# A one-core transformer step: six PSUM banks in turn in the merge and the output projection, norm diagonals on ScalarE, statistics of the second norm two slices later

## The chip, the cores and the metric

The kernel runs on one NeuronCore of a Trainium2 chip. The metric is the device time of one launch in microseconds (us), lower is better. Before the change three timed runs gave 1827.52, 1832.23 and 1832.83 us; their median is 1832.23 us.

## What is computed

One trunk layer of a hybrid diffusion backbone in fp32, for 128 context tokens and 1024 latent tokens (1152 in all), width 1024:

```
h   = rmsnorm(x, w1) * (1 + scale1) + shift1
q, k, v, u, g = h @ w_in                     # 4 heads, differential attention; conv input u; gates g
attn = head_norm(softmax(q1 k1) v - lam * softmax(q2 k2) v) @ w_attn_proj
conv = silu(layernorm(dwconv31(glu(u)))) @ w_conv_proj
m   = sigmoid(g[:1024]) * attn + sigmoid(g[1024:]) * conv
x   = x + gate1 * (m @ w_out)
h   = rmsnorm(x, w2) * (1 + scale2) + shift2
up  = dwconv3(h @ w_up)                      # 2 x 2816 channels
x   = x + gate2 * ((silu(up[:2816]) * up[2816:]) @ w_down)
y   = rmsnorm(x, w_final)
```

The six modulation vectors come from `silu(c) @ w_ada + b_ada`, for the context and for the latent conditioning.

## The kernel before

**Layout.** Activations stand transposed: 128 channels on the partitions, tokens along the row. The 1152 tokens are cut into three column groups n = 0, 1, 2 of 384 (CH). A tensor of width 1024 is eight chunks k of 128 channels.

**Matmuls.** To keep fp32 accuracy every operand is split in a high and a low part; `mm3` (line 196) issues three matmuls per chunk (high x high, high x low, low x high). One output block of 128 x 384 is a *unit*: 24 matmuls over eight chunks. The weights stream in a fixed order: SyncE (SP) loads a raw tile, ScalarE (ACT) makes the high part (line 153), GpSimd (POOL) the low part (line 155).

**PSUM.** There are eight banks. `banks` (line 284) makes the tags f (two banks), T (two) and O (one), and S (three banks in one tile). In attention S holds the scores. `any5` (line 293) hands out f, T, O, f, T in turn. At the start of `merge` (line 1043) one S tile is taken as `spare`: `spare[:, 0]` becomes `self.st`, the bank for norm statistics, and `spare[:, 1:3]` is a junk output for a reduction (`ada2`, line 1152).

**Ticks.** `run` (line 209) advances a clock, one tick after every eight matmuls of a unit (`mm3`'s yields, three ticks a unit of the output projection). `defer(t, f)` calls f at the tick now + t, so the number decides where in the written order the instructions of f stand. After that the framework's planner, which simulates the engines with its own costs, may still move instructions: an instruction that it thinks is not ready lets later ones pass. `pin` (line 296) bounds how far (on PE 144 places, on DVE 24).

**A norm's statistics.** Four steps: `stat_cols` (line 218) sums squares over the partitions with tiny matmuls into a PSUM bank, VectorE (DVE) adds EPS (line 228, tile `ms`), POOL takes the power -1/2 (line 230, `rs`). `stat_diag` (line 234) multiplies the 128 x 128 identity by one column of `rs` per 128 tokens (line 238, tile `dg`, up to three instructions). `stat_bcast` (line 242) multiplies a matrix of ones by `dg`, which puts the row of factors on all partitions in a PSUM bank. The consumers then read that bank. `stat_diag` serves the first norm (three groups), the conv layernorm in the last half of attention (`ln_jobs`, five groups, nine instructions in all), the second norm (three) and the final norm (three): 36 instructions.

**Merge** (lines 1084 to 1127). For each of eight output chunks j and each n: 12 matmuls into one bank (conv part), 12 into the next (attention part). DVE multiplies each by its gate tile `tg` (line 1110) and adds them (line 1112), ACT makes the high part `mh` (line 1114), POOL the low part `ml` (line 1116; DVE for j = 7). `tg` has two buffers; the load for the slice two further on is issued on SP's queue after that (line 1118), since it overwrites the buffer which `ml` has just read. Between the slices DVE runs `ada2` (line 1159): reductions over 1024 elements that make the later modulation vectors.

**Output projection** (`wo_unit`, line 1236). First pass: for j = 0..7 the units of n = 0 and 1. After each unit DVE adds the gated result to x1 (`resid`, line 1186), ACT squares it (line 1196) and DVE adds the square to `acc[n]` (line 1197). Second pass: j = 0..7 for n = 2. In the second pass the statistics and the normalisation of n = 0 and 1 are slipped in with `defer` (line 1261): a = `stat_cols`, a2 = `stat_diag`, b = `stat_bcast`, c0..c3 = `modnorm` (line 249: DVE multiplies, lines 253 and 261, ACT makes the high part, line 259, DVE and POOL the low part, line 267). Then the MLP (`ffn_body`, line 1273) begins, and n = 2 is normalised in its first units. The MLP's results go through ACT (line 1284) to `up`, and DVE's depthwise conv reads them (lines 1289 and 1291).

Of the kernel before, what the change touches and what calls it, by code (L numbers as in the profile page):

```python
# [10 lines left out]
AF = mybir.ActivationFunctionType  # L11
ALU = mybir.AluOpType
# [68 lines left out]
def _w_order():  # L81
    order = ["q0", "k0", "ua0", "ub0", "ua1", "ub1", "v0", "v1", "v2", "v3"]
    fill = FILL_SEQ.split()
    tail = [f"g{i}" for i in range(16) if f"g{i}" not in fill]
    merge = [f"m{j}" for j in range(8)]
    wo = [f"wo{j}" for j in range(8)]
    ffn = []
    done = 0
    for i in range(NFF):
        ffn += [f"fa{i}", f"fb{i}"]  # L90
        if i >= 2 and i % 2 == 0 and i < NFF - 2:
            ffn += [f"d{done}_0", f"d{done}_1"]
            done += 1
    while done < NFF // 2:
        ffn += [f"d{done}_0", f"d{done}_1"]
        done += 1
    return order, fill, tail, merge, wo, ffn
# [15 lines left out]
class Kernel:  # L113
# [120 lines left out]
    def stat_diag(self, rs, nt):  # L234
        nc = self.nc
        dg = self.sm.tile([128, CH], F32, tag="dg", name="dg", bufs=2)
        for t in range(nt):
            nc.vector.tensor_scalar(out=dg[:, t * 128:(t + 1) * 128], in0=self.ident,
                                    scalar1=rs[:, t:t + 1], scalar2=None, op0=ALU.mult)
        return dg  # L240

    def stat_bcast(self, dg, nt, psum):
# [41 lines left out]
    def banks(self, pool):  # L284

        def tag(t, n):
            return lambda: pool.tile([128, 512], F32, tag=t, name=t, bufs=n)

        self.fps, self.tps, self.ops = tag("f", 2), tag("T", 2), tag("O", 1)
        self.sps = lambda: pool.tile([128, 3, 512], F32, tag="S", name="S")  # L290
        self.five = cycle((self.fps, self.tps, self.ops, self.fps, self.tps))

    def any5(self):
        return next(self.five)()
# [748 lines left out]
    def merge(self):  # L1043
        tc, nc, A = self.tc, self.nc, self.A
        mh = [None] * NCH
        ml = [None] * NCH
        with tc.tile_pool(name="p2", bufs=1) as p2:
# [3 lines left out]
                xl.append(p2.tile([128, 8, CH], F32R, name=f"col{n}"))  # L1051

            self.gate_tile = lambda: self.sm.tile([128, CH], F32, tag="dg", name="gate", bufs=2)
            fps = self.any5
            spare = self.sps()
            self.st = lambda: spare[:, 0]
            self.junk = spare[:, 1:3]

            with tc.tile_pool(name="p2a", bufs=1) as p2a:
# [24 lines left out]
            with tc.tile_pool(name="p2b", bufs=1) as p2b:  # L1084
# [13 lines left out]
                for j in range(KC):  # L1098
                    wh, wl = self.take(f"m{j}")
                    for n in range(NCH):  # L1100
# [8 lines left out]
                        for s, ps in ((1, pc), (0, pa)):  # L1109
                            nc.vector.scalar_tensor_tensor(out=tg[:, s], in0=tg[:, s], scalar=1.0, in1=ps[:, :CH],  # L1110
                                                           op0=ALU.add, op1=ALU.mult)
                        nc.vector.scalar_tensor_tensor(out=tg[:, 0], in0=tg[:, 1], scalar=0.5, in1=tg[:, 0],
                                                       op0=ALU.mult, op1=ALU.add)
# [52 lines left out]
    def out_and_ffn(self):  # L1166
        tc, nc, A = self.tc, self.nc, self.A
        vec = self.vec
        with tc.tile_pool(name="p3", bufs=1) as p3:
            x1 = [p3.tile([128, KC, CH], F32, name=f"x1_{n}") for n in range(NCH)]  # L1170

            def load_x(n, q):
                nc.scalar.dma_start(out=x1[n][:, 2 * q:2 * q + 2], in_=A["xT"][n][:, 2 * q:2 * q + 2])

            load_x(0, 0)
            load_x(1, 0)

            fps, st = self.any5, self.st

            def bc8(v):  # L1180
                return v.rearrange("p (k o) -> p k o", o=1).to_broadcast([128, KC, 2])

            def resid(n, j, ps, gate):
                for o, ln, c in self.segs(n):
                    d = x1[n][:, j, o:o + ln]
                    nc.vector.scalar_tensor_tensor(out=d, in0=ps[:, o:o + ln], scalar=gate[:, j, c:c + 1], in1=d,  # L1186
                                                   op0=ALU.mult, op1=ALU.add)

            acc = [p3.tile([128, CH], F32, name=f"acc{n}") for n in range(NCH)]

            def square(n, j):
                if j == 0:
                    nc.scalar.activation(out=acc[n], in_=x1[n][:, 0], func=AF.Square)
                else:
                    sq = self.sm.tile([128, CH], F32, tag="dg", name="sq", bufs=2)
                    nc.scalar.activation(out=sq, in_=x1[n][:, j], func=AF.Square)
                    nc.vector.tensor_tensor(out=acc[n], in0=acc[n], in1=sq, op=ALU.add)

            hh = [None] * NCH
            hl = [None] * NCH  # L1200

            flip = [0]

            def mn():
                flip[0] += 1
                t = p3a.tile([128, 1156], F32, tag=("ya", "yb")[flip[0] % 2], name="mn")
                return t[:, :2 * CH].rearrange("p (k t) -> p k t", k=2)

            def h2(n, pool):
                hh[n] = self.hb.tile([128, KC, CH], F32R, tag="hb", name=f"h2h{n}")  # L1210
                hl[n] = self.hb.tile([128, KC, CH], F32R, tag="hb", name=f"h2l{n}")
                box = {}

                def a():
                    box["rs"] = self.stat_cols(acc[n], 3, st)

                def b():
                    box["r"] = self.stat_bcast(box["dg"], 3, st)

                def c(q):  # L1220
                    def f():
                        self.modnorm(n, 2 * q, 2, x1[n], box["r"][:, :CH], self.s2, self.h2s, hh[n], hl[n], pool,
                                     lambda i: i == 1 and n < 2)
                    return f

                def a2():
                    box["dg"] = self.stat_diag(box["rs"], 3)
                return [a, a2, b] + [c(q) for q in range(4)]

            with tc.tile_pool(name="p3a", bufs=1) as p3a:  # L1230
                self.start_ada2([p3a.tile([128, T], F32R, tag="fh", name=f"cbd{c}", bufs=4)[:, :1024].bitcast(F32)
                                 for c in range(2)],
                                lambda: p3a.tile([128, T], F32R, tag="fl", name="araw", bufs=4)[:, :1024].bitcast(F32))
                self.ada_fetch(2)

                def wo_unit(j, ns):
                    wh, wl = self.take(f"wo{j}")
                    for n in ns:
                        ps = fps()
                        self.run(self.mm3(ps[:, :CH], self.unit_ops(wh, wl, n, self.mh, self.ml), 8))  # L1240
                        resid(n, j, ps, self.g1)
                        square(n, j)
                        if n == ns[0]:
                            self.prep_to(self.late_prep)

                for j in range(KC):
                    if j % 2 == 0 and j < 6:
                        load_x(0, j // 2 + 1)
                        load_x(1, j // 2 + 1)
                    if j >= 4:  # L1250
                        load_x(2, j - 4)
                    wo_unit(j, (0, 1))
                    for _ in range(2):
                        if self.ada_raw:
                            self.ada2(1, self.ada_fetched < 24)
                nc.vector.tensor_copy(self.h2s, self.mod[:, 1])
                nc.vector.tensor_scalar(out=self.s2, in0=self.mod[:, 2], scalar1=1.0, scalar2=None, op0=ALU.add)
                nc.vector.tensor_tensor(out=self.s2, in0=self.s2, in1=bc8(vec[:, V_N2:V_N2 + 8]), op=ALU.mult)
                st0, st1 = h2(0, mn), h2(1, mn)
                for i, f in enumerate(st0 + st1):  # L1260
                    self.defer(1 + i + i // 2, f)
                for j in range(KC):
                    wo_unit(j, (2,))
                self.fetch_ahead = 2
                self.flush()
                for i, f in enumerate(h2(2, mn)):
                    self.defer(i // 2 + 1, f)
                self.ada_fetch(2)
                self.bg = [lambda: self.ada2(1)] * 8 + [lambda: nc.vector.tensor_copy(self.g2, self.mod[:, 3])]
                self.bg_rate = (1, 5)  # L1270
                self.ffn_body(p3, fps, st, x1, hh, hl, resid, square, acc, p3a)
# [289 lines left out]
```

## Time and profile before

| | us |
|---|---|
| median of three runs | 1832.23 |
| profiled execution, its own time | 1829.33 |
| span of the profiled execution, first to last instruction | 1827.2 |
| PE busy | 1723.0 (94%) |
| DVE busy | 1206.4 (66%) |
| POOL busy | 719.0 (39%) |
| ACT busy | 605.2 (33%) |

PE is TensorE, whose weight loads (PEld) run beside the matmuls; DVE is VectorE, ACT ScalarE, POOL GpSimd, SP SyncE. "idle <- X" names what the engine waited for last. The span is cut below into stages by time: the merge lies at 742 to 866 us, the output projection at 856 to 971 us, the MLP from there to the end.

### The profile page before, as it was taken

What the parts mean: (1) busy time and instruction counts of PE and PEld (TensorE: products, weight loads), DVE (VectorE), ACT (ScalarE), POOL (GpSimd) and SP (SyncE); (2) the same over time, 40 slices, a digit from 0 to 9 for tenths busy, and PEclk for the clock granted to TensorE, in tenths of its full rate; (3) what the DMA queues carried; (4) which work ended last, traced back from release to release, by engine and by line L of the source; (5) the groups of instructions that cost most, each with busy time, mean ns of one, the idle gap of its engine ahead of it and who ended that gap; (6) DMA issues with size and microseconds to landing.
All of it is one profiled execution on the core that took longest, in us unless ns stands there. A gap on an engine that the chain in (4) does not pass through costs nothing.

```text
span 1827.2 us, 25202 instructions
## 1 busy us (share of the span) xinstructions
PE 1723.0 (94%) x10138; PEld 1681.9 (92%) x10138; DVE 1206.4 (66%) x1515; ACT 605.2 (33%) x1097; POOL 719.0 (39%) x466
## 2 busy tenths in 40 slices
PE   5989889989989999899989999999999999999997
PEld 3889889988989999889989999999999999999997
DVE  5868985697796663687888855463554535545466
ACT  4424444354454553311243312222121221221222
POOL 2545782673873422644353422222222322322231
PEclk8999999999999999899999999999999999999998
DMA  8264233423325424665832211111111111111102
GB/s 312 80 186 143 91 94 88 151 78 118 116 76 184 138 87 166 224 212 176 283 113 58 93 35 47 43 39 47 37 46 47 35 47 47 35 47 47 35 24 104
DMA packets 86172, 184.05 MB, mean 101 GB/s; under 512 B 8196, under 2 KB 56232, under 8 KB 84008
## 3 DMA queue, kind: packets, MB, share of 16 engines
q1 hardware_dynamic: 33888, 101.27, 17.0%
q10 hardware_dynamic: 51592, 79.08, 13.6%
q0 software_dynamic: 576, 2.10, 0.3%
q8 instruction: 80, 1.31, 0.3%
q14 instruction: 36, 0.29, 0.1%
HBM read 142.80 MB, written 39.60 MB: 100 GB/s over the span
## 4 chain that ended last, share of the span: by engine, by line
PE 58%; DVE 19%; issue 5%; POOL 4%; DMA 2%; ACT 2%; ACTq 0%; POOLq 0%; DVEq 0%
PE f L203 25%; PE T L203 19%; PE O L203 9%; DVE conv L611 6%; DVE S L1159 2%; DVE mx L753 2%; PE O L794 2%; DVE e L766 2%; DMA tg<-scr_gscr 2%; DVE atl L783 1%; PE T L779 1%; PE S L746 1%; PE S L747 1%; POOL ml L1116 1%; POOL wlo L155 1%
## 5 line engine op out<-in xcount | busy, mean ns | idle before, releaser
L155 POOL TENSOR_TENSOR wlo<-raw,whi 128x1024 fp32r<-128x1024 f32 x123 | 311.5, 2534 | 619.8 <-ACT whi L153 518.2
L203 PE MATMUL f<-h1h,whi 128*128 128x384 f32 x680 | 232.6, 344 | 4.7 <-ACT gt L574 3.4
L203 PE MATMUL f<-h1l,whi 128*128 128x384 f32 x680 | 233.7, 344 | 0.0
L203 PE MATMUL f<-h1h,wlo 128*128 128x384 f32 x680 | 230.9, 340 | 0.0
L153 ACT CAST whi<-raw 128x1024 fp32r<-128x1024 f32 x125 | 131.0, 1048 | 283.9 <-PE f L203 114.7
L611 DVE SCALAR_TENSOR_TENSOR conv<-glu,vec,conv 128x967 f32<-128x967 f32 x120 | 199.2, 1660 | 1.1
L1289 DVE TENSOR_SCALAR ya<-up,vec 128x1153 f32<-128x1153 f32 x22 | 54.1, 2459 | 175.7 <-ACT up L1284 175.7
L203 PE MATMUL T<-h2h,whi 128*128 128x384 f32 x432 | 144.3, 334 | 0.0
L203 PE MATMUL T<-h2l,whi 128*128 128x384 f32 x432 | 144.3, 334 | 0.0
L203 PE MATMUL T<-h2h,wlo 128*128 128x384 f32 x432 | 144.1, 334 | 0.0
L624 POOL TENSOR_TENSOR conv<-conv,tap 128x200 f32<-128x200 f32 x120 | 115.6, 963 | 68.4 <-ACT tap L618 65.9
L203 PE MATMUL f<-h2h,whi 128*128 128x384 f32 x416 | 139.7, 336 | 2.6 <-ACT up L1284 2.6
L203 PE MATMUL f<-h2h,wlo 128*128 128x384 f32 x416 | 139.5, 335 | 0.0
L203 PE MATMUL f<-h2l,whi 128*128 128x384 f32 x416 | 139.3, 336 | 0.0
L203 PEld LDWEIGHTS f<-h1h,whi 128*128 128x128 f32 x680 | 129.5, 191 | 6.8 <-ACT gt L574 4.1
L203 PEld LDWEIGHTS f<-h1l,whi 128*128 128x128 f32 x680 | 130.1, 191 | 0.4
L203 PEld LDWEIGHTS f<-h1h,wlo 128*128 128x128 f32 x680 | 129.3, 190 | 0.2
L1305 POOL TENSOR_TENSOR fl<-ya,fh 128x128 fp32r<-128x128 f32 (+1 forms) x44 | 64.9, 1476 | 154.1 <-ACT fh L1304 154.1
L753 DVE TENSOR_REDUCE mx<-S 128x1 f32<-128x1152 f32 (+1 forms) x72 | 88.7, 1231 | 31.1 <-PE S L747 31.1
L1186 DVE SCALAR_TENSOR_TENSOR x<-f,g,x 128x384 f32<-128x384 f32 (+2 forms) x154 | 74.9, 505 | 48.6 <-PE f L203 45.5
L755 ACT ACTIVATE e<-S,mx 128x1152 f32<-128x1152 f32 (+1 forms) x72 | 81.2, 1128 | 70.1 <-DVE mx L753 62.7
L1289 DVE TENSOR_SCALAR yb<-up,vec 128x1153 f32<-128x1153 f32 x22 | 54.3, 2469 | 70.6 <-ACT up L1284 70.6
(332 smaller groups left out, 4646.3 us busy)
## 6 DMA issues: line engine op xcount, KB each, us to landing
raw<-in_wst SPq DMA_DIRECT2D x126, 512.0 KB, 3.5
araw<-in_ada ACTq DMA_DIRECT2D x32, 512.0 KB, 3.9
scr_gscr<-gate ACTq DMA_DIRECT2D x48, 192.0 KB, 2.0
tg<-scr_gscr SPq DMA_DIRECT2D x24, 384.0 KB, 4.1
ada<-in_ada SPq DMA_DIRECT2D x8, 1024.0 KB, 9.9
K<-scr_kscr ACTq DMA_DIRECT2D x4, 1920.0 KB, 8.8
V<-scr_vscr ACTq DMA_DIRECT2D x4, 1280.0 KB, 6.5
scr_vscr<-e ACTq DMA_DIRECT2D x36, 128.0 KB, 1.9
```

The costliest lines, as they stand in the source:

```text
L153: nc.scalar.copy(hi, raw)
L155: eng.tensor_tensor(out=lo, in0=raw, in1=hi.bitcast(F32), op=ALU.subtract)
L203: nc.tensor.matmul(out, lhsT=a, rhs=b, start=(i == 0), stop=(i == n - 1))
L611: t = nc.vector.scalar_tensor_tensor(out=o, in0=glu[:, j:j + CSPLIT], scalar=w[:, j:j + 1], in1=o, op0=ALU.mult, op1=ALU.add)
L624: t = nc.gpsimd.tensor_tensor(out=o, in0=o, in1=p, op=ALU.add)
L753: nc.vector.tensor_reduce(out=mx[:, 1:2], in_=src, axis=AX.XY, op=ALU.min)
L755: nc.scalar.activation(out=e[:, :w].rearrange("p (a b) -> p a b", a=nk), in_=src, func=AF.Exp, scale=-1.0, bias=mx[:, 1:2], accum_out=self ...
L766: nc.vector.scalar_tensor_tensor(out=e0[:, :w], in0=e1[:, :w], scalar=m1[:, 3:4], in1=e0[:, :w], op0=ALU.mult, op1=ALU.add)
L794: nc.tensor.matmul(o_ps[:, :w], lhsT=a, rhs=b, start=(i == 0), stop=(i == n - 1))
L1186: nc.vector.scalar_tensor_tensor(out=d, in0=ps[:, o:o + ln], scalar=gate[:, j, c:c + 1], in1=d, op0=ALU.mult, op1=ALU.add)
L1289: nc.vector.tensor_scalar(out=y[:, :L], in0=u[:, 0:L], scalar1=w[:, 0:1], scalar2=None, op0=ALU.mult)
L1305: nc.gpsimd.tensor_tensor(out=fl[:, d:d + ln], in0=ya[:, s:s + ln], in1=fh[:, d:d + ln].bitcast(F32), op=ALU.subtract)
```

## The change

Four edits. (1) `stat_diag` makes the diagonals with a ScalarE activation (Copy with a per-partition scale) instead of a VectorE multiply, in all 36 places. (2) A cycle `six` of f, T, O, f, T and `spare[:, 0]` hands out the accumulation banks from the end of the gate projections to the end of the output projection. (3) In the output projection the statistics and the broadcast of the second norm for n = 0 and 1 take their banks from that same cycle instead of always `spare[:, 0]`; before the MLP both names go back to what they were. (4) The deferred steps for n = 0 and 1 come two ticks later.

```diff
     def stat_diag(self, rs, nt):
...
-            nc.vector.tensor_scalar(out=dg[:, t * 128:(t + 1) * 128], in0=self.ident,
-                                    scalar1=rs[:, t:t + 1], scalar2=None, op0=ALU.mult)
+            nc.scalar.activation(out=dg[:, t * 128:(t + 1) * 128], in_=self.ident, func=AF.Copy,
+                                 scale=rs[:, t:t + 1])
...
+    def any6(self):
+        return next(self.six)()
...
-            fps = self.any5
             spare = self.sps()
             self.st = lambda: spare[:, 0]
+            self.six = cycle((self.fps, self.tps, self.ops, self.fps, self.tps, self.st))
+            fps = self.any6
             self.junk = spare[:, 1:3]
...
-            fps, st = self.any5, self.st
+            fps, st = self.any6, self.any6
...
                 for i, f in enumerate(st0 + st1):
-                    self.defer(1 + i + i // 2, f)
+                    self.defer(3 + i + i // 2, f)
                 for j in range(KC):
                     wo_unit(j, (2,))
                 self.fetch_ahead = 2
                 self.flush()
+                fps, st = self.any5, self.st
```

## Rows read from the trace of the kernel before

**Rows 1.** The page: busy us of each engine, its share of the span, instructions.
```profile
PE 1723.0 (94%) x10138; PEld 1681.9 (92%) x10138; DVE 1206.4 (66%) x1515; ACT 605.2 (33%) x1097; POOL 719.0 (39%) x466
```

**Rows 2.** Busy time of each engine by stage: stretch, its length, then busy us (instructions) of PE, PEld, DVE, ACT, POOL, then granted clock, DMA share, GB/s.
```profile
590.00:710.00 120.00, 118.60 (x763) 117.09 (x762) 72.64 (x111) 63.93 (x122) 37.97 (x39) 1.00 0.33 105
742.00:866.00 124.00, 111.16 (x600) 107.07 (x599) 95.54 (x144) 25.79 (x38) 57.18 (x34) 0.96 0.59 191
886.00:927.00 41.00, 38.18 (x221) 37.86 (x219) 39.23 (x60) 9.51 (x15) 14.06 (x5) 1.00 0.62 200
927.00:965.00 38.00, 32.37 (x175) 31.75 (x176) 30.85 (x46) 17.03 (x30) 23.37 (x13) 0.89 0.34 99
965.00:1022.00 57.00, 54.25 (x310) 53.61 (x309) 49.91 (x69) 21.52 (x36) 18.94 (x10) 0.98 0.20 60
1022.00:1068.00 46.00, 43.56 (x235) 41.99 (x236) 39.98 (x42) 13.00 (x25) 15.58 (x8) 0.97 0.20 69
1068.00:1780.00 712.00, 711.09 (x4089) 708.36 (x4089) 368.28 (x443) 159.94 (x270) 193.63 (x98) 1.00 0.14 41
```

**Rows 3.** What PE's matmuls waited for between 700 and 1000 us: us in total, times, longest.
```profile
PE S L246 <- DVE dg L238: 5.4, 2, 3.9
PE f L203 <- DVE tg L1110: 5.0, 4, 1.8
PE f L203 <- ACT gate L577: 4.7, 1, 4.7
PE S L225 <- DVE acc L1197: 3.2, 2, 3.1
PE T L203 <- DVE tg L1110: 3.0, 3, 1.6
```

**Rows 4.** What DVE waited for between 700 and 1000 us: us in total, times, longest.
```profile
DVE tg L1110 <- DMA tg<-scr_gscr: 20.8, 12, 4.4
DVE mn L253 <- PE S L246: 7.5, 2, 3.8
```

**Rows 5.** The merge's gate loads and one turn of their loop. First the DMA's issues (count, KB each, median us to landing), then the timeline: start us, duration us, engine, line, instruction.
```profile
tg<-scr_gscr SPq DMA_DIRECT2D x24, 384.0 KB, 4.1
821.37 0.55 DVE L1110 SCALAR_TENSOR_TENSOR tg<-tg,f 128x384 f32<-128x384 f32 x1 [4.45 <-DMA tg<-scr_gscr]
824.69 1.44 POOL L1116 TENSOR_TENSOR ml<-tg,mh 128x384 fp32r<-128x384 f32 x1 [4.32 <-ACT mh L1114]
```

**Rows 6.** Timeline of DVE at the end of the merge.
```profile
859.09 0.55 DVE L1116 TENSOR_TENSOR ml<-tg,mh 128x384 fp32r<-128x384 f32 x1
863.27 0.55 DVE L1110 SCALAR_TENSOR_TENSOR tg<-tg,f 128x384 f32<-128x384 f32 x1 [2.02 <-DMA tg<-scr_gscr]
```

**Rows 7.** Timeline around the first broadcast of the second norm (n = 0), in order of time, DVE, PE and POOL.
```profile
923.32 2.04 DVE L1197 TENSOR_TENSOR acc<-acc,sq 128x384 f32<-128x384 f32 x1 [0.65 <-ACT sq L1196]
927.27 0.83 PE L225 MATMUL S<-cols,acc 128*128 128x1 f32 x6 [3.09 <-DVE acc L1197]
930.59 0.87 POOL L230 TENSOR_TENSOR rs<-ms,cols 128x3 f32<-128x3 f32 x1 [0.56 <-DVE ms L228]
931.49 0.68 DVE L238 TENSOR_SCALAR dg<-cst,rs 128x128 f32<-128x128 f32 x3 [0.98 <-POOL rs L230]
```

**Rows 8.** A piece of the chain that ended last, followed back from 965 us: start us, us, what.
```profile
935.85 0.67 PE S L246 x6
```

**Rows 9.** Timeline around the second broadcast (n = 1).
```profile
957.19 0.85 POOL L230 TENSOR_TENSOR rs<-ms,cols 128x3 f32<-128x3 f32 x1
957.50 1.03 ACT L153 CAST whi<-raw 128x1024 fp32r<-128x1024 f32 x1
958.02 4.63 POOL L155 TENSOR_TENSOR wlo<-raw,whi 128x1024 fp32r<-128x1024 f32 x2
958.08 4.85 DVE L238 TENSOR_SCALAR dg<-cst,rs 128x128 f32<-128x128 f32 x3 [1.10 <-POOL rs L230]
962.79 1.22 PE L246 MATMUL S<-dg,ones 128*128 128x128 f32 x4 [1.51 <-DVE dg L238]
965.05 1.81 DVE L253 TENSOR_TENSOR mn<-x,S 128x768 f32<-128x768 f32 x2
```

**Rows 10.** Two stretches of the second pass by the same columns as rows 2: after the wait for acc and after the wait for dg.
```profile
927.30:932.90 5.60, 5.60 (x25) 5.60 (x26) 3.85 (x7) 1.75 (x4) 3.26 (x2) 0.70 0.34 113
960.40:967.10 6.70, 5.10 (x17) 4.81 (x18) 6.05 (x9) 1.59 (x3) 2.25 (x1) 0.51 0.53 160
```

**Rows 11.** Durations by shape: ACT groups with their count, busy us and mean ns, and all instructions of line 238 on DVE (ns min/median/max, first and last start).
```profile
L618 ACT ACTIVATE tap<-glu,vec 128x200 f32<-128x200 f32 x120 | 55.5, 462 | 105.3 <-POOL conv L624 90.4 <-issue 3.0 <-DMA scr_vscr<-e 2.6
L800 ACT ACTIVATE ot<-O 128x128 f32<-128x128 f32 x4 | 1.1, 276 | 3.1 <-PE O L794 3.1
L259 ACT ACTIVATE h2h<-mn,h2s,s 128x128 fp32r<-128x128 f32 x8 | 3.9, 484 | 1.4 <-DVE mn L253 1.4
L238 DVE TENSOR_SCALAR dg<-cst,rs x36: 273/282/2376, 17.6 to 1817.9; 128x128 f32<-128x128 f32 x36
  POOL rs L230: 11.0, 11
```

**Rows 12.** Timeline: ACT when the first diagonals of the launch are made, and PE at the last broadcast of the launch.
```profile
17.50 1.82 ACT L388 ACTIVATE sq<-x 128x768 f32<-128x768 f32 x2
1817.84 1.65 PE L246 MATMUL f<-dg,ones 128*128 128x128 f32 x6 [1.51 <-DVE dg L238]
```

## The prediction

> **What bounds the kernel now.** I read the page first, then busy time by stage, the waits of PE and of DVE, and last the timeline at each wait that the change touches. The page gives PE 94% of the span, so 104 us are left without a matmul [rows 1]; the question is which of them this change can reach. The stages tell [rows 2]: from 1068 to 1780 us PE is busy 711.09 of 712 us, and from 590 to 710 us 118.60 of 120, so nothing can be won there. Between 742 and 1068 us PE idles some 30 us, and in most of that stretch DVE is as full as PE: 39.23 of 41 us (886 to 927), 49.91 of 57 (965 to 1022), 39.98 of 46 (1022 to 1068). PE's waits name the places [rows 3]: 8.0 us for `tg` in the merge (5.0 + 3.0), 4.7 us for the last gate evacuation, 3.2 us for `acc` and 5.4 us for `dg` in the output projection. The reader is to see that PE's wait is a symptom: each ends when DVE has done something, so I follow DVE.
>
> **Six banks in the merge: 0 us.** One more bank lets PE run 12 matmuls further ahead, 12 x 0.174 = 2.1 us (0.174 is 711 us over 4089 matmuls [rows 2]). It helps only if DVE then finishes earlier. DVE itself stands 20.8 us in 12 waits for the `tg` load [rows 4]. One turn of that loop shows it [rows 5]: DVE reads at 821.37 after 4.45 us of waiting; `ml` ends at 824.69 + 1.44 = 826.13; only then may the buffer be loaded again, 4.1 us to landing by the median. From read to next read that is 826.13 - 821.37 + 4.1 = 8.9 us for two slices, against 48 matmuls x 0.174 = 8.35 us of PE. So the loop is slower than PE, holds no PSUM bank, and sets the end of the merge: the last slice is read at 863.27, again after a wait for the load [rows 6]. With six banks PE reaches the output projection up to 2.1 us earlier and there meets the low part of chunk 7, made at 859.09 [rows 6]: its wait moves, it does not go. The same bank shortens the 4.7 us wait at the merge's start [rows 3], with the same end. Bounds: 0, and 8.0 us if all waits for `tg` went. I take 0, as the loop rows are the nearest. The bank that statistics now share with units costs nothing I can see: a bank comes round after six uses, some five units of 24 x 0.174 = 4.2 us, and the broadcast is read out within about 11 us.
>
> **Two ticks later.** PE's statistics matmul for n = 0 waits 3.09 us for `acc`, issued at 927.27 [rows 7]. Two ticks are 16 matmuls, 16 x 0.174 = 2.8 us of work that PE does meanwhile, so about 0.3 us of the wait is left; `acc` itself is no earlier, since DVE is full before it. What is won is the clock behind the wait: the next 5.60 us ran at a granted 0.70 [rows 10], a mixture of the two levels 1.2 and 2.4 GHz, and at the full level they take 5.60 x 0.70 = 3.9 us, 1.7 us less. The broadcast of n = 0 stands on PE's queue at 935.85 [rows 8], behind this stretch, with `dg` ready since 931.49 + 0.68 = 932.17 [rows 7], and DVE waits for it (one of the two waits in the 7.5 us of [rows 4]). So the whole normalisation of n = 0 starts 1.7 us earlier. Bounds: 0, if the planner puts more matmuls between statistics and broadcast, and 3.0, where the new `dg` sets it (below).
>
> **Diagonals on ACT.** The trace has no such operation, so I bound it by its neighbours: 276 ns (128 columns, constant scale) and 484 ns (128 columns, scale and bias per partition) [rows 11]. Nearest is the tap multiply, a Copy with a scale per partition like the new one, 462 ns at 200 columns; with 72 columns fewer I take 0.40 us, an estimate between the two ends. Three are 1.2 us, against 0.68 us on an undisturbed DVE [rows 7]. For n = 0: `rs` ends at 931.46, `dg` at about 932.7, or 933.7 behind a weight cast of 1.03 us; the broadcast stands later on PE's queue anyway, cost 0. For n = 1 DVE took 4.85 us for three [rows 9], with POOL's two weight subtractions running from 958.02 to 962.65, beside 0.68 without. `rs` is ready at 957.19 + 0.85 = 958.04, and ACT is occupied by a cast until 958.53, so on ACT the three end at 959.2 to 959.7 in the old times, 3.2 to 3.7 us before 962.93. The broadcast then ends some 1.1 us later (the last four matmuls took 1.22), and DVE, which in the old run had first to catch up and started `mn` at 965.05 [rows 9], can start at about 960.9: 4.1 us earlier. With the 1.7 us from the tick shift that is **5.8 us** by which the normalisation of n = 1, and behind it `acc` and the statistics of n = 2, move forward. PE's own wait at this broadcast may stay several us long, since PE gets there earlier; that costs nothing as long as DVE sets the pace. The tick shift itself delays nothing: all fourteen deferred steps still fall within the 24 ticks of the second pass (the last at 3 + 13 + 6 = 22). To 1068 us DVE stays full [rows 2], and from then on PE, so the 5.8 us arrive at the end.
>
> The Trainium skill, "SBUF — State Buffer", section "Who interferes with whom", says that DVE and GpSimd share one port pair as an exclusive lock, that a DVE instruction with two SBUF inputs also meets it, and that ScalarE never waits there. The trace agrees with the first part: 4.85 us instead of 0.68 beside POOL's subtractions [rows 9]. By this rule the lock finds another victim on DVE; what that would do here is the second rival.
>
> **Other diagonals.** Conv layernorm (nine): PE has 1.4 us of idle left in that stretch [rows 2], so a gain is at most 1.4; a loss is the third rival; taken 0. First norm: ACT runs squares at 17.50 for 1.82 us [rows 12], three diagonals ahead of them delay them by 1.2 us, while DVE is relieved of 0.68; bounds -0.7 and +1.2, taken +0.4. Final norm: the last broadcast waits 1.51 us for `dg` and starts after the first of three [rows 12], so only one instruction's difference counts, 0.40 - 0.28 = +0.1.
>
> **Sum.** -5.8 + 0.4 + 0.1 = -5.3 us. The profiled execution took 1829.33 us (span 1827.2, 2.1 around it): 1824.0. The median of the runs, 1832.23, lies 2.9 above it, and from there the sum gives 1826.9. I say 1825.5, between the two.
>
> **Rivals.**
> 1. *The merge does gain.* The 8.0 us of waits for `tg` go with the sixth bank, on top of the forecast: 1825.5 - 8.0 = 1817.5. For it: five waits of up to 1.8 us are each shorter than the 2.1 us that a bank buys [rows 3]. Against: DVE never waits for PE there, but 20.8 us for the load [rows 4].
> 2. *The port takes the next victim.* With `dg` gone, POOL's subtractions run beside DVE's `acc` sum and `mn`. The `acc` sum took 2.04 us beside one of them and 0.56 alone [rows 7]; two such are 3.0 us, and the weight cast ahead of the diagonals 0.5 to 1.0 more. Then 5.8 shrinks to about 2: around 1829.5, not to be told from before. The same comes out where the planner undoes the two ticks.
> 3. *ACT's queue is held (slower).* ACT works in order. A diagonal waiting for POOL's `rs` holds the exponentials, evacuations and weight casts behind it. DVE waited 11.0 us for `rs` before its diagonals [rows 11]; ACT takes that over, and 36 x 0.40 = 14.4 us of work. If half of these 25.4 us reaches PE, +12.7 us, and with the gain of 5.3 lost to the same queue the run takes about 1842; it is slower than before once some 11 us arrive, and near 1838 with two thirds of that in conv layernorm and first norm. For it: PE waits for the exponentials already and has no reserve there. Against: ACT is busy only 63.93 of 120 us in that stretch [rows 2].
>
> The Trainium skill, "ScalarE: Activation LUTs", section "Rules for kernel authors", speaks for the third: it sends multiplications to VectorE. The rows bear it out per instruction (0.40 estimated against 0.28) and not beside POOL (up to 2.38 [rows 11]).
>
> **Chances.** Forecast 0.45 (own range 1821 to 1830), first rival 0.18, second 0.24, third 0.13. A measurement of this kernel tells about 0.3%, 5.5 us, from no change, so "faster" begins below 1826.7. The forecast sits near that edge: 0.27 of its 0.45 count as faster, 0.18 as the same. With the first rival (0.18 faster), the second (0.03 faster, 0.21 same) and the third (0.02 same, 0.11 slower) this makes 0.48, 0.41 and 0.11. The range reaches from 1815, where the first rival gains a little more than its sum, to 1834, past the second; most of the third is left out.
>
> **What would show it.** Right: the wait of PE for `acc` falls from 3.09 to under 1 us and the clock stays full behind it; the n = 1 diagonals on ACT take about 1.2 us; `mn` of n = 1 starts some 5 to 6 us earlier measured from the end of `acc`; waits for `tg` on DVE stay near 20 us, with a new PE wait at the first units of the output projection. Wrong: PE's waits for `tg` vanish and the merge's last read comes earlier (first rival); sums and multiplications of the second norm take 2 us each around the second broadcast (second); ACT shows idle before `dg` with exponentials queued behind (third).

## The result, and the profile after

The change makes the kernel slower: 1849.01 us (median of 4 runs) against 1829.88 before in the same set, a ratio of 1.0113 with a 95% interval of 1.0087 to 1.0138. Forecast were 1825.5 us, with a range to 1834. The profiled execution took 1848.09 us, 18.8 more than the one of before. In the new kernel the lines from the bank pool on have moved by 3 to 5. One execution each of e4 and e14 below ran at a granted clock of 0.75 and took 2103.29 and 2092.74 us; these two are left out of their medians and ratios.

The stages first, with the columns of [rows 2]; the third is the same work as the last of [rows 2], 15.3 us later.

```profile
590.00:710.00 120.00, 119.17 (x767) 118.16 (x766) 66.87 (x98) 67.37 (x130) 40.98 (x38) 1.00 0.32 104
742.00:869.00 127.00, 111.68 (x611) 107.19 (x612) 86.74 (x135) 26.63 (x40) 55.95 (x34) 0.97 0.58 188
1083.30:1795.30 712.00, 711.09 (x4089) 708.33 (x4090) 368.30 (x442) 160.13 (x270) 193.56 (x98) 1.00 0.14 41
```

In the steady part PE is busy for the same 711.09 us, and the first phase ends where it did: the merge begins at 735.91 us, before at 735.87. To place the loss I read four times from each trace's timeline: the first matmul on `coh` or `col` (merge begins), the first and the last on `mh`/`ml` (output projection), the last of the first down projection, and the end of the last instruction. The lengths between them, in us, for all runs, each from one profiled execution, whose own time lies up to 5.8 us above (e8) or 2.9 below (e6) the median of its kernel; the ratio is from all executions:

| kernel | merge | output projection | to end of first down | both | rest | ratio to before (95%) |
|---|---|---|---|---|---|---|
| before | 120.2 | 115.4 | 109.7 | 225.2 | 742.6 | |
| the change | 122.9 | 124.5 | 113.2 | 237.7 | 746.0 | 1.0113 |
| e1 diagonals alone | 124.4 | 111.0 | 111.7 | 222.6 | 745.0 | 1.0032 (1.0020 to 1.0044) |
| e2 two slices later alone | 119.6 | 110.2 | 112.1 | 222.2 | 742.6 | 0.9988 (0.9978 to 0.9997) |
| e3 six banks alone | 131.4 | 127.8 | 111.8 | 239.6 | 742.6 | 1.0132 (1.0117 to 1.0147) |
| e4 sixth bank its own tile | 138.6 | 105.3 | 116.0 | 221.3 | 744.0 | 1.0077 (1.0054 to 1.0099) |
| e5 and splits held back | 122.6 | 107.7 | 115.1 | 222.8 | 744.9 | 1.0028 (1.0016 to 1.0039) |
| e6 own tile, merge on five | 123.5 | 106.6 | 114.4 | 221.0 | 744.4 | 1.0015 (1.0006 to 1.0025) |
| e7 as e6, diagonals on DVE | 120.8 | 114.9 | 108.9 | 223.8 | 742.6 | 0.9988 (0.9978 to 0.9997) |
| e8 the change without six | 126.4 | 106.2 | 116.6 | 222.8 | 745.7 | 1.0031 (1.0020 to 1.0043) |
| e9 diagonals of conv norm | 124.1 | 114.7 | 109.7 | 224.4 | 742.6 | 1.0013 (1.0003 to 1.0022) |
| e10 diagonals of last norm | 120.1 | 116.5 | 109.7 | 226.2 | 746.7 | 1.0030 (1.0020 to 1.0039) |
| e11 second norm, both edits | 120.4 | 105.6 | 116.0 | 221.6 | 742.4 | 0.9978 (0.9968 to 0.9988) |
| e12 as e11, six in projection | 121.7 | 106.9 | 114.4 | 221.3 | 742.5 | 0.9985 (0.9976 to 0.9995) |
| e13 as e11, no last modulation | 120.4 | 106.2 | 106.6 | 212.8 | 742.6 | 0.9930 (0.9910 to 0.9949) |
| e14 as e11, one slice later | 120.0 | 108.0 | 116.9 | 224.9 | 742.6 | 0.9977 (0.9966 to 0.9987) |
| e15 as e11, six in both | 121.4 | 107.1 | 114.9 | 222.0 | 741.8 | 0.9994 (0.9985 to 1.0004) |

The change loses 2.7 us in the merge, 12.6 in the output projection and the first units behind it, and 3.5 at the end: 18.8. The waits name the main place. PE between 700 and 1000 us, to be held against [rows 3] (us in total, times, longest):

```profile
PE T L203 <- DVE x L1190: 8.4, 2, 5.1
PE T L203 <- DVE tg L1114: 5.6, 5, 1.7
PE f L203 <- DVE tg L1114: 2.6, 3, 1.8
PE T L203 <- DVE col L1075: 2.3, 1, 2.3
```

The waits for `dg` and nearly all for `acc` of [rows 3] are gone, as forecast, and a new one stands first: PE waits for `x`, the residual that gives an output bank back. DVE in the same stretch, to [rows 4]:

```profile
DVE tg L1114 <- DMA tg<-scr_gscr: 31.5, 15, 4.0
DVE x L1190 <- PE S L203: 20.9, 3, 12.7
```

So PE waits for DVE, and DVE for PE, 12.7 us in one piece, for a unit on bank S, the new sixth one. DVE's timeline shows what stands around that wait:

```profile
895.35 1.29 DVE L1163 CUSTOM_DVE_ANT_0 S<-araw,cbd,vec 128x1024 f32<-128x1024 f32 x1 [0.33 <-DMA araw<-in_ada]
896.73 1.29 DVE L1163 CUSTOM_DVE_ANT_0 S<-araw,cbd,vec 128x1024 f32<-128x1024 f32 x1
897.94 0.61 DVE L1190 SCALAR_TENSOR_TENSOR x<-T,g,x 128x384 f32<-128x384 f32 x1
898.47 2.97 DVE L1163 CUSTOM_DVE_ANT_0 S<-araw,cbd,vec 128x1024 f32<-128x1024 f32 x1
...
901.54 1.29 DVE L1163 CUSTOM_DVE_ANT_0 S<-araw,cbd,vec 128x1024 f32<-128x1024 f32 x1
...
915.56 0.74 DVE L1190 SCALAR_TENSOR_TENSOR x<-S,g,x 128x128 f32<-128x128 f32 x2 [12.67 <-PE S L203]
```

The reductions of the modulation (line 1163) also write to `S`: their unused output lies in `spare[:, 1:3]`, the sixth bank is `spare[:, 0]`, and both are one tile. PE runs that unit only from here:

```profile
911.20 0.33 PE L203 MATMUL S<-mh,whi 128*128 128x384 f32 x1
```

It is the first unit of the second column. Two units precede it in the code, and ten in the trace (244 matmuls by then, 24 to a unit): PE comes to it after the four reductions that the code has between the first column and the second, and DVE stands before its result while `f`, `T` and `O` units wait to be read.

That unit is not all. The longest of PE's waits for `x`, 5.1 us, stands 20 us earlier:

```profile
880.69 0.74 DVE L1190 SCALAR_TENSOR_TENSOR x<-f,g,x 128x128 f32<-128x128 f32 x2
891.11 0.69 PE L203 MATMUL T<-mh,whi 128*128 128x384 f32 x1 [5.13 <-DVE x L1190]
```

The first of these two is the first residual. It comes 21.8 us after the first matmul of the projection, in the kernel before 13.0 (869.07 against 856.07): eight reductions of the merge now stand on DVE behind the read of the merge's last unit on S (862.18) and ahead of it. So reductions wait for units on S, as units wait for reductions.

### The profile page after: what moved, and what is told of

It reads as the page before. It is cut to its first block, busy times and chain, and to the rows that moved or that the text cites. A ratio compares the mean times of both kernels' runs of the same rounds, so it can differ in the third digit from the quotient of the medians.

```text
span 1846.0 us, 25188 instructions
## 1 busy us (share of the span) xinstructions
PE 1730.5 (94%) x10138; PEld 1685.0 (91%) x10138; DVE 1181.9 (64%) x1479; ACT 616.3 (33%) x1133; POOL 724.2 (39%) x466
## 5 line engine op out<-in xcount | busy, mean ns | idle before, releaser
L203 PE MATMUL T<-h2h,whi 128*128 128x384 f32 x416 | 140.4, 338 | 4.9 <-ACT up L1289 4.4
L203 PE MATMUL f<-h2h,whi 128*128 128x384 f32 x432 | 144.2, 334 | 0.7 <-DVE x L1190 0.7
L203 PE MATMUL f<-h2l,whi 128*128 128x384 f32 x432 | 144.5, 335 | 0.1
L203 PE MATMUL f<-h2h,wlo 128*128 128x384 f32 x432 | 144.4, 334 | 0.2 <-POOL wlo L155 0.2
L203 PE MATMUL T<-h2l,whi 128*128 128x384 f32 x416 | 140.3, 337 | 0.0
L203 PE MATMUL T<-h2h,wlo 128*128 128x384 f32 x416 | 139.9, 336 | 0.0
L1190 DVE SCALAR_TENSOR_TENSOR x<-T,g,x 128x384 f32<-128x384 f32 (+2 forms) x148 | 72.6, 509 | 46.3 <-PE T L203 46.0
```

Of the source, the lines that this page charges most:

```text
L203: nc.tensor.matmul(out, lhsT=a, rhs=b, start=(i == 0), stop=(i == n - 1))
```

## The experiments

Theory A said that this shared tile is the loss. Its rivals were ScalarE's queue (B) and the luck of any new order (C). Four kernels, each with one difference.

**e1, diagonals alone** (the first hunk of the diff on the kernel before).

> The kernel before with one edit of the change: the norm diagonals made on ScalarE. Theory A (shared tile: the sixth bank lies in the same three-bank tile as the two banks into which the reductions of the modulation write their unused output, so a unit on it is put in order with the reductions, and the loss of 18 us comes from that): this edit has no part in the loss, 1826 to 1832 us, the part that I had forecast for it being a gain of about 4. Theory B (ScalarE's queue is held by the twelve copies that now wait for the mean square, and evictions and squares behind them come late): most of the loss is here, 1840 to 1848 us. Theory C (any edit shifts the order in which the scheduler puts the units, and the loss is the luck of an order): some microseconds in either direction, 1820 to 1840, with places that differ from those of the whole change.

**e2, statistics alone** (`self.defer(1 + ...)` to `3 + ...`).

> The kernel before with one edit: the statistics of the second norm two slices later. Theory A: 1826 to 1831 us, nothing or a small gain from the 3 us wait on the last accumulated square that goes. Theory B: as A, since ScalarE's queue is untouched. Theory C: some microseconds off in either direction, up to 1840.

**e3, six banks alone** (the other hunks).

> The kernel before with one edit: six banks in turn in the merge and in the output projection, the sixth from the tile of the unused outputs. Theory A: nearly the whole loss is here, 1843 to 1849 us, with the units on the sixth bank some ten units behind their turn in the output projection and a VectorE wait for them of some 20 us in sum. Theory B: no loss, 1826 to 1832 us. Theory C: between 1825 and 1845, and not where the whole change loses.

**e4, the whole change with a tile of its own.**

```diff
-            spare = self.sps()
-            self.st = lambda: spare[:, 0]
+            self.st = self.sts
-            self.junk = spare[:, 1:3]
...
+                    self.sts = lambda: pt.tile([128, 512], F32, tag="st", name="st", bufs=1)
+                    self.junk = pt.tile([128, 2, 512], F32, name="junk")
```

> The whole change, but the sixth bank is a tile of its own, apart from the two banks of the unused outputs (both in a pool that is opened for the second phase alone). Theory A: the units on the sixth bank come in their turn, VectorE doesn't wait for them, and the time is that which I forecast or near it, 1822 to 1831 us. Theory B: the loss stays, 1843 to 1849 us, since ScalarE still makes the diagonals. Theory C: the loss changes by some microseconds but doesn't go, 1834 to 1848.

Measured: 1833.27, 1824.93, 1852.26 and 1844.74 us, before 1827.23 in that set. B falls as the explanation of the whole: without the diagonals e3 loses more than the change. That PE's units on S wait for reductions, which write to the other two banks, stands as a row of e3 (700 to 1000 us; `mod` is the stored sum of a reduction):

```profile
PE S L203 <- DVE mod L1163: 7.1, 6, 3.9
```

But e1 loses 6 us of its own, which A had not, and e3 and e4 lie above A's ranges. C is not out: what follows is about orders. A is right and not enough: with its own tile the output projection and the stretch behind it fall from 237.7 to 221.3 us (the column "both"), PE's waits in the projection fall to 1.9 us, the first residual comes 12.4 us after its first matmul and not 21.8, and yet e4 is hardly faster, since its merge takes 138.6. Stages of e4, merge first:

```profile
736.80:875.40 138.60, 114.36 (x578) 109.84 (x578) 99.82 (x136) 27.07 (x39) 63.03 (x34) 0.91 0.56 182
875.40:980.70 105.30, 103.31 (x601) 102.43 (x601) 85.48 (x123) 38.70 (x64) 45.27 (x29) 1.00 0.59 197
```

ScalarE's waits in that merge have rows that the kernel before has only once, for 1.0 us:

```profile
ACT whi L153 <- PE O L203: 16.2, 6, 4.5
ACT whi L153 <- PE T L203: 7.0, 1, 7.0
```

The timeline of ScalarE and GpSimd in one turn, and the DVE instruction that `mh` needs:

```profile
791.29 0.51 ACT L1121 CAST mh<-tg 128x384 fp32r<-128x384 f32 x1 [6.28 <-DVE tg L1119]
...
794.49 0.56 DVE L1119 SCALAR_TENSOR_TENSOR tg<-tg 128x384 f32<-128x384 f32 x1
796.30 1.05 ACT L153 CAST whi<-raw 128x1024 fp32r<-128x1024 f32 x1 [4.50 <-PE O L203]
797.26 0.51 ACT L1121 CAST mh<-tg 128x384 fp32r<-128x384 f32 x1
...
797.43 2.40 POOL L155 TENSOR_TENSOR wlo<-raw,whi 128x1024 fp32r<-128x1024 f32 x1 [4.13 <-ACT whi L153]
799.79 2.00 POOL L1123 TENSOR_TENSOR ml<-tg,mh 128x384 fp32r<-128x384 f32 x1
```

The slab split `whi` waits for PE to give a weight buffer back; `mh` behind it, whose input DVE had ready at 794.49 + 0.56 = 795.05, starts 2.2 us late; `ml` stands behind `wlo`, and only after `ml` is the gate buffer loaded again. In the order of ScalarE's instructions `mh` of a column's first slice comes ahead of the split in the kernel before, and behind it in e4, for every column. My reading, which no run shows directly: with six banks the scheduler, which sorts by its own estimate of when things are ready, takes the split for ready one slice sooner. Two theories: this order (D), or PE running ahead (E).

**e5, e4 with the order of before written out**, without a semaphore: `c` and `d` are the split of a slab on ScalarE and GpSimd, `prev` the evictions `mh` and `ml` of the first slice, a column earlier.

```diff
+            for i, a in zip((c, d), self.behind):
+                self.tc.add_manual_dep(i.ins, a.ins.name, NOSYNC, reason="order")
...
+                            self.behind = prev
                             self.prep_to(self.late_prep)
+                            prev = (mhc, mlc)
```

> The whole change with the sixth bank as a tile of its own (as in the run before), and in the merge one pair of orders more, without a semaphore: a weight slab is split on ScalarE and GpSimd only behind the evictions (mh, ml) of the first slice of the column three slabs earlier, where the kernel before has it too; with six banks the scheduler had put it one slice ahead of them. Theory D (the merge of the last run lost 18 us because the split waits in ScalarE's queue for TensorE to give a weight buffer back, and the evictions behind it, and with them the reloads of the gate buffers, come late): the merge takes 119 to 125 us in place of 138.6, and the output projection keeps its 105, so 1822 to 1832 us. Theory E (six banks do it by themselves: TensorE runs further ahead, the same waits come in fewer and longer pieces, and its clock falls in them): the merge stays above 130 us, 1836 to 1846 us.

**e6, e4 with five banks in the merge** (`fps = self.any5` there).

> The whole change with the sixth bank as a tile of its own, but the merge on five banks; only the output projection takes six. Theory D: the scheduler leaves the splits behind the evictions, the merge takes 119 to 125 us and the output projection about 105, so 1820 to 1832 us, as the run with the order written out. Theory E: the same here, so that this run is 10 us or more faster than that one.

**e7, e6 with the diagonals on VectorE.**

> As the run with five banks in the merge and six in the output projection, but with the norm diagonals left on VectorE. If what the diagonals cost alone (6 us: 2.4 in the last stretch, 4 at the start of the merge) adds up with the rest, this is 4 to 7 us faster than it, 1814 to 1824 us; if the diagonals on ScalarE take waits away in the output projection here, as I had forecast, it is equal or slower.

**e8, the change without the sixth bank** (e1 and e2 together).

> The change without the sixth bank: diagonals on ScalarE and statistics two slices later. If the two add up as each alone (1.0032 and 0.9988), 1830 to 1833 us, 3 us slower than before. By my forecast, in which these two take about 5 us out of the second norm, 1821 to 1825 us. Both say that the 18 us of the whole change need the sixth bank.

Measured: 1831.72, 1830.79, 1824.72 and 1831.96 us against 1827.33. The merge of e5:

```profile
736.60:859.20 122.60, 107.42 (x578) 100.88 (x577) 94.14 (x134) 27.21 (x39) 60.43 (x35) 0.99 0.61 206
```

122.6 in place of 138.6 us by two order edges per column: D holds, E falls, and six banks (e5) and five (e6, 123.5) come out alike to about a microsecond. e7 is 6.1 us faster than e6 by the medians; in the profiles it gains 2.7 us in the merge and 1.8 at the end, and is 8.3 slower in the projection, as I had forecast of the diagonals, but gets 5.5 of that back behind it. The two profiled executions are only 2.5 us apart, as that of e6 is one of its fastest. e8 (1.0031, 1.0020 to 1.0043) is e1 and e2 together at the edge of its interval (1.0032 x 0.9988 = 1.0020); so of the change's 1.0113 some 0.008, or 15 us, come with the sixth bank.

What do the diagonals cost? All runs with them everywhere have a merge of 122.6 to 126.4 us (e4 aside) and 744 to 746 us at the end; those without have 119.6 to 120.8 and 742.6 (e3's merge aside: there the weight splits wait 30.1 us in sum for units on S and O, two of them ahead of the first `mh` of their column as in e4, and PE waits 6.0 us for reductions). So I put them to one place at a time.

**e9, conv norm only; e10, last norm only; e11, second norm only, with e2; e12, e11 with six banks in the projection.** Each passes a flag to `stat_diag`.

```diff
-                box["dg"] = self.stat_diag(box["rs"], 3)
+                box["dg"] = self.stat_diag(box["rs"], 3, True)
```

> The kernel before with the norm diagonals on ScalarE only in the norm of the convolution, in the first phase. Theory F (the 4 us that the merge lost with all diagonals on ScalarE come from the order at its start: the scheduler now puts the copy of the second slice's convolution half, coh, behind two gate evictions that wait for a buffer): merge 123 to 126 us against 120.2, all the rest as before, 1829 to 1833 us. Theory G (the diagonals of the second norm do it, by ScalarE's queue in the merge or behind it): nothing here, 1826 to 1829 us.

> The kernel before with the diagonals on ScalarE only in the last norm. If the last stretch lost its 2.4 us (742.6 to 745.0 us from the end of the first down projection) by these: 745 here, merge 120, and 1828.5 to 1831 us. If it lost them by something earlier: no change, 1826 to 1828.5 us.

> The kernel before with the statistics two slices later, and the diagonals on ScalarE only in the second norm, the place for which I had forecast the gain. If the losses of the diagonals lie at the other places: merge 120, last stretch 742.6, and the output projection with the stretch behind it 222 to 224 us against 225.2, so 1822 to 1826 us. By my forecast for these two edits: 1821 to 1823 us. If the second norm's diagonals cost something themselves: 1827 us and more.

> What is left of the change without the places that cost: statistics two slices later, diagonals on ScalarE in the second norm only, six banks in the output projection only, the sixth a tile of its own. Output projection and the stretch behind it 221 us as in the same with all diagonals, merge 120, last stretch 742.6: 1820 to 1825 us. If the sixth bank is worth nothing beside five, equal to the run with five banks within 2 us.

Measured: 1830.37, 1832.75, 1824.50 and 1825.42 us against 1827.70. F's place holds: e9's merge is 3.9 us longer, and no other stage by more than 0.8 off; by the medians the whole is 2.7 us longer. ScalarE at the merge's start, first before, then e9 (merge begins at 735.87 and 733.68):

```profile
734.58 1.48 ACT L1070 CAST coh<-col 128x1536 fp32r<-128x1536 f32 x1 [0.71 <-DMA col<-scr_cvscr]
735.96 0.48 ACT L577 ACTIVATE gate<-f 128x384 f32<-128x384 f32 x1
...
737.87 0.48 ACT L577 ACTIVATE gate<-T 128x384 f32<-128x384 f32 x1
```

```profile
734.88 0.49 ACT L581 ACTIVATE gate<-f 128x384 f32<-128x384 f32 x1 [1.98 <-DMA scr_gscr<-gate]
735.96 0.49 ACT L581 ACTIVATE gate<-T 128x384 f32<-128x384 f32 x1 [0.58 <-PE O L203]
736.85 1.48 ACT L1074 CAST coh<-col 128x1536 fp32r<-128x1536 f32 x1 [0.40 <-ACT gate L581]
```

`coh` of the second slice has moved behind two gate evictions that wait for a buffer and a matmul, so it comes 4.5 us later, counted from the merge's start (+3.17 against -1.29), and PE goes on behind its long wait there after 14.6 us and not after 11.1 (748.30 and 746.98 in the timelines). The diagonals themselves, the last of them made at 694 us, wait for nothing here: they changed the order. That the later copy makes the 3.9 us is read from these timelines and not tested, since no run put it back with the diagonals left on ScalarE. In e15 below it is as late (+3.5) without these diagonals, on six banks, and the merge takes 121.4.

In the last norm (e10) it is 4.1 us, by the medians 5.0, more than the 2.4 looked for. PE and DVE, first before, then e10 (the last down matmul begins at 1813.89 and 1811.89):

```profile
1804.18 0.83 PE L246 MATMUL S<-dg,ones 128*128 128x128 f32 x6
1805.05 5.34 DVE L1379 SCALAR_TENSOR_TENSOR x<-x,vec,S 128x384 f32<-128x384 f32 x10
1810.31 0.61 DVE L1186 SCALAR_TENSOR_TENSOR x<-T,g,x 128x384 f32<-128x384 f32 x1
1814.07 2.26 PE L225 MATMUL T<-cols,sqf 128*128 128x1 f32 x18
```

```profile
1805.99 0.83 PE L250 MATMUL S<-dg,ones 128*128 128x128 f32 x6
1807.07 5.33 DVE L1383 SCALAR_TENSOR_TENSOR x<-x,vec,S 128x384 f32<-128x384 f32 x10
1812.32 0.61 DVE L1190 SCALAR_TENSOR_TENSOR x<-T,g,x 128x384 f32<-128x384 f32 x1
1814.50 3.92 PE L225 MATMUL T<-cols,sqf 128*128 128x1 f32 x18 [2.28 <-DVE sqf L1415]
```

The broadcast of the middle slice comes 9.7 us before the last down matmul in the one, 5.9 in the other. The ten scalings behind it end 3.5 us before that matmul there and 0.5 us after it here, with the last residuals, squares and sums behind them on DVE. So the 18 statistics matmuls of the last slice wait 2.28 us and take 3.92, where the kernel before starts them at once and takes 2.26. e11 is the fastest of these four, 0.9978; the sixth bank (e12, 0.9985) adds nothing.

The second norm's two edits take 9.8 us out of the projection in e11 and bring 3.6 in the column "both". e13 and e14 asked what takes the rest; e15 asked for the sixth bank with every order mended.

**e13, without the last modulation's reductions; e14, `defer(2 + ...)`; e15, e5 with the diagonals as in e11.**

> The run with the second norm's diagonals on ScalarE and its statistics two slices later, and without the sixteen reductions of the last modulation vector, which stand on VectorE between the output projection and the first down projection (its gate is copied from another part; this leaves that vector uncomputed). They are 16 x 1.42 = 23 us of VectorE. Theory H (VectorE's work sets when the first down projection ends, so what the output projection gains is waited for there): the stretch from the last output matmul to the end of the first down projection falls from 116 to 104 to 109 us, 1811 to 1818 us. Theory I (it is set by when the second norm's halves are ready and by TensorE's own work): 114 to 116 us, 1821 to 1825 us.

> The run with the second norm's diagonals on ScalarE, but its statistics one slice later in place of two. Theory I: the 4 us in which TensorE waited for the norm's halves at the start of the first units (up to 2.2 us for h2l, 1.5 for h2h) go, and the wait for the last square stays away, 1820 to 1823 us. Theory H: the sum of output projection and the stretch behind it stays at 221 to 223 us, 1822 to 1826 us.

> The change with its places mended: six banks in both stretches with the sixth a tile of its own, the weight splits held behind the evictions in the merge, statistics two slices later, diagonals on ScalarE in the second norm only. If six banks are worth nothing in the merge once the order is right, as I had forecast, it is within 2 us of the run with five banks (1824.5 us in its set): 1822 to 1827 us, merge 119 to 123 us. If TensorE running further ahead pays or costs: below 1820 or above 1829.

Measured: 1816.06 (two executions), 1823.75 and 1827.10 us against 1827.83. The stretch behind the projection, and PE's waits for the norm's halves in it, e11 and then e13:

```profile
960.70:1076.70 116.00, 107.10 (x590) 103.77 (x589) 97.05 (x126) 36.25 (x63) 36.12 (x20) 0.97 0.19 64
PE f L203 <- DVE h2l L271: 2.4, 2, 2.2
PE f L203 <- ACT h2h L263: 1.5, 1, 1.5
```

```profile
960.50:1067.10 106.60, 102.53 (x590) 101.05 (x590) 74.80 (x94) 36.02 (x63) 36.06 (x20) 1.00 0.16 50
PE f L203 <- DVE h2l L271: 2.5, 2, 2.1
PE f L203 <- ACT h2h L263: 1.5, 1, 1.5
```

With 22 us of DVE's work gone the stretch is 9.4 us shorter and the granted clock is 1.00: H holds. The waits for the halves are the same in both, so I, that they set the stretch, falls. They may have a part, though: the kernel before has none of them, and in e11 they make 3.9 us, in a stretch that is 6.3 us longer than its. Two things stay open. e13 also lacks the loads that feed the reductions, for one of which DVE waits 3.7 us in e11, so loads and reductions are not told apart. And e14 decides nothing: the waits did not go (3.1 us for `h2l`), its column "both" has 224.9, above the 221 to 223 of H, and its ratio (0.9977) is that of e11. e15 is some 3 us slower than e11 by the ratios (0.9994 against 0.9978), where I had allowed 2; no stage of it differs by more than 1.5 us, so the place is not shown.

## Why the prediction was wrong

**Six banks in the merge.** The arithmetic held: the loop over the gate buffers sets the merge, and where the order is kept a sixth bank is worth nothing (e5 against e6; e15 against e11, 121.4 and 120.4). What I left out is that the loop's steps share queues with the weight splits, and that more banks change the scheduler's order of these. In e4 that is the whole 16 us. In the change the splits happen to stay behind `mh` as before, and the 2.7 us are less than the 3.9 that the merge lost with the conv diagonals alone. DVE's wait for the load was to stay near 20 us; it went to 31.5 [rows 4].

**The step that failed** is the sentence that the bank which statistics now share with units "costs nothing I can see". I asked how long a bank is in use. I didn't ask what else lies in its tile: the reductions write to the other two banks of it, and units were sorted behind reductions that never touch their bank, and reductions behind units. Cost: 237.7 against 221.3 us with the tile split (e4), some 16 us, where I had 0.

**Two ticks later.** Right for n = 0: the `acc` wait of 3.09 us [rows 7] is 0.6 in e11, and e2 gains (0.9988).

**Diagonals on ACT** in the second norm. The price is right: three take 0.99 us where I had estimated 1.2 from [rows 11]. The projection falls from 110.2 (e2) to 105.6 us (e11), 4.6, but that this lies near my 4.1 is luck, for my 4.1 was another thing, the earlier start of `mn` of n = 1 on DVE. From PE's first statistics matmul to this `mn` it is 37.8 us in the kernel before [rows 7] [rows 9], 38.9 in e2 and 36.0 in e11. So the tick shift brings it no earlier, the diagonals 2.9 us, and both together 1.8, where I had 5.8. In e11:

```profile
926.59 0.83 PE L225 MATMUL S<-cols,acc 128*128 128x1 f32 x6 [0.62 <-DVE acc L1201]
957.08 0.99 ACT L239 ACTIVATE dg<-cst,rs 128x128 f32<-128x128 f32 x3
957.17 5.05 POOL L155 TENSOR_TENSOR wlo<-raw,whi 128x1024 fp32r<-128x1024 f32 x2
958.51 1.46 DVE L1201 TENSOR_TENSOR acc<-acc,sq 128x384 f32<-128x384 f32 x1 [2.78 <-ACT sq L1200]
960.56 2.08 DVE L1201 TENSOR_TENSOR acc<-acc,sq 128x384 f32<-128x384 f32 x1
962.56 1.80 DVE L257 TENSOR_TENSOR mn<-x,S 128x768 f32<-128x768 f32 x2
```

The diagonals are ready at 958.07, but two sums stand ahead of `mn` on DVE, and beside POOL's subtractions they take 1.46 and 2.08 us, where the same sum takes 0.54 at 962.86 in the kernel before. What the projection won are mostly waits of PE, and the larger of them I had priced at nothing: its 5.4 us for `dg` [rows 3] are 0.3 in e11.

"The 5.8 us arrive at the end" was wrong as well: I read DVE as full to 1068 us [rows 2] and took that as a reason for the gain to be kept. DVE's work there is the reason why most of it is not. PE comes to the first units sooner, DVE still has the same work ahead of the first down projection, and 6.3 of 9.8 us are lost again there (e11, e13).

**Other diagonals.** Mis-sized: conv norm 0, measured 3.9 in its stage (e9); last norm +0.1, measured 4.1 (e10). I priced the instruction (0.40 against 0.28, which is right) and not its place in the order. For the first norm nothing is left: the other three account for e1 (1.0013 x 1.0030 x 0.9978 / 0.9988 = 1.0033, e1 has 1.0032), to within some 4 us by the intervals. The beginning of the merge tells less, as it scatters from 731.7 to 737.6 us over the kernels.

**Rivals.** The first, that the waits for `tg` go, is out: they are 8.2 us, before 8.0. The second, DVE's sums slowed beside POOL, is not the loss, but in the second norm it came true: it said that the 5.8 us shrink to about 2, and the rows of e11 above show 1.8, with the sums beside POOL as it said. The third had the sign, and "ACT's queue is held" is what e4 shows, but by weight splits and not by diagonals waiting for `rs`; the price came from a place that none of the three named. The Trainium skill's rule that I had set behind it ("ScalarE: Activation LUTs", "Rules for kernel authors": multiplications to VectorE) would have kept the conv and last norms as they were, where it pays (3.9 and 4.1 us in e9 and e10); in the second norm e11 against e2 shows no loss by not keeping it.

Open: why the scheduler's estimate moves `coh` and the last broadcast when diagonals move to ScalarE was not tried; the runs show that it does, where, and what it costs.

## What to carry to other kernels

Before a spare buffer gets a second use, look at the tile that it is cut from: order is kept for the tile, and an unrelated writer next to it can hold a whole unit. Where a scheduler sorts the instructions, an edit's price has two parts, the instruction and the new order; compare each in-order queue's order of before and after, and write out the edges that must stay. A gain in a stretch counts only if the engine that sets the next one has room: ask what that engine still has to do before the next fixed point.

## What I had not expected of the hardware

After a wait of 3.20 us in e4's merge the next matmuls came 0.32 us apart, as at the lower of the two clock levels (1.2 GHz), and for 6 us; then 0.17, as at 2.4 GHz:

```profile
789.15 0.69 PE L203 MATMUL T<-coh,whi 128*128 128x384 f32 x1 [3.20 <-DVE tg L1117]
789.64 0.52 PE L203 MATMUL T<-col,whi 128*128 128x384 f32 x1
...
795.39 0.34 PE L203 MATMUL O<-col,whi 128*128 128x384 f32 x1
```

The granted clock was 0.50 from 789.15 to 795.40 us. So the long waits of this merge cost twice: its granted clock was 0.91 over all, and 0.99 in e5.

The reduction of 2.97 us among those of 1.29, shown with the result, is no accident. POOL's weight subtraction ran beside it from 897.96 to 900.36, and the reduction ended 1.09 us after it. In the change eight of the 64 reductions took 1.50 to 3.48 us, and each ended 1.09 us after a subtraction of POOL that was running when it began; in the kernel before it is 13 of 64, with the same 1.09.
